# A hybrid attention / linear-recurrence step on one core: row sums traced in halves, eight casts moved to GpSimd, and eighteen products of the output projection listed inside the attention

## The chip, the cores and the metric

The kernel runs on one core of one Trainium2 chip. The core has five engines that run beside each other and are joined by semaphores: TensorE (PE, matrix products; PEld is its weight load), VectorE (DVE), ScalarE (ACT), GpSimd (POOL) and SyncE (SP, which here only issues DMAs). Every engine works its instructions off in the order of its own queue. [...]

The metric is the device time of one launch in microseconds. Three runs of the kernel before gave 846.48, 842.91 and 846.51 us, median 846.48.

## The reference, cut to what matters

Two layers work on 640 tokens: 512 latent tokens and 128 context tokens. Layer 0 is gated attention, layer 1 a gated linear recurrence. The change touches layer 0 and the hand-over to layer 1.

```python
# layer 0 (attention), for context (p) and latent (s) tokens
sh, sc, g = split(silu(cond) @ ada_w[0] + ada_b[0], 3)      # per-layer shift, scale, gate
h = x * (1 + sc) + sh
q, k, v, gate = split(h @ attn_w_in, [1024, 1280, 1536])     # 16 heads of 64, 4 key/value heads
q, k = rms_norm(q), rms_norm(k)                              # and rotary positions for s
p = softmax(q k^T / 8); o = p v                              # s reads 128 cached + 512 own keys
out = (o * silu(gate)) @ attn_w_out                          # the output projection, 1024 x 1024
x = layer_norm(ALPHA * x + g * out)
# layer 1 (recurrence) begins with its own modulation
sh, sc, g = split(silu(cond) @ ada_w[1] + ada_b[1], 3)
h1 = x * (1 + sc) + sh
```

All matrix products are made to nearly fp32 accuracy out of three products of reduced operands: an operand `x` is split into `hi = round(x)` and `lo = x - hi`, and `x w` becomes `hi hi + hi lo + lo hi`.

## The kernel before, in words

**Tiles.** 640 tokens are five tiles of 128 (tile 4 is the context). A width of 1024 is eight blocks `k` of 128. Activations `hhi`, `hlo` lie with the features on the partitions; after the attention the same two tiles hold the split, gated attention output.

**Weights.** Every weight piece is 128 x 1024, loaded by SP into a ring of three raw buffers (`rawp`), at most two pieces ahead (`pump`, L197). `split_piece` (L232) turns it into `hi` (L240, a cast on ACT) and `lo` (L241, a subtraction with two SBUF inputs, on DVE for all pieces that matter here). The loads are pinned: SP issues them in the order of the program, and one that waits for a buffer holds up all later ones.

**Order of the work.** All up to the output projection's weights stands in one block (L168 to L1248) that a list scheduler orders: for each engine it picks, at each simulated time, among the instructions whose inputs are there and whose buffers are free. `keep_in_program_order` pins an instruction behind the one traced before it on its engine. `issue_after(ins)` adds an order edge to `ins` from each instruction of its body that is on the engine of `ins`.

**Lead-in** (`lead_in`, L753). After keys, values and the first of four query chunks, 16 steps (L846 to L864) make the gate columns `gs`: each step is a half tile of 24 products (`gps`, L349 to L351) and a SiLU on ACT (L854). Beside them run the first chunk's query work (`q_job`: `qn` L615, rotary L654 to L658, split `qs` L693 and L694, transposes `qps` L702) and the *row sums* (`ada_cols`, L331): layer 1's shift and scale are 16 jobs, each of two DVE instructions (L335) that multiply a 128 x 1024 piece of `ada_w` with a row of silu(cond) and sum along the row. Twelve jobs run in the lead-in, one a step, from a ring of two buffers (`adar`, loads L840), their products spilled into `gs`; four run in `cols_gen` (L340) beside the first later query chunk, from `rawp`, spilled into the ring `s2` of two buffers that `q_split` (L689) takes its tiles from as well.

**Attention** (`att_gen`, L1001). 36 units, nine for each of four chunks `c`: eight sample units (one head, 256 queries) and one prompt unit. A unit's front (L959) is four score products (`sc`, L869 and L870), a maximum on DVE (L964), an exponential on ACT (L969) and, some steps later, a reciprocal on DVE (L974) and the scaling of the probabilities on POOL (L975). Its back is ten transposes (L982), copies out of PSUM (L874), and for two units together 20 products with the values (`pot`, L896) and the gating on DVE (L901). Fronts run two units ahead. The side work (`Side`, L60) is woven in at 0.62 steps per step of the attention: query chunks 1 to 3 (`q_gen`, L713) with the row sums or the gate rows (`ada_gen`, L315, products `adaps` L284), then the split of the first four output pieces (`prefetch_gen`, L1117) and the split of the attention output (`split_gs`, L1109).

**Output projection and first norm.** `out_mms` (L1153) makes 24 products of 128 x 512 for a token tile and a half `nh` of the columns; the loop at L1387 runs tiles and halves as (0,0), (1,0), (0,1), (1,1), (2,0), ... `Norm.half` (L1170) multiplies by the gate, adds the residual and takes statistics, `Norm.finish` scales, `h1_tile` (L1250) transposes the tile for layer 1. The PSUM pool of this phase (`Phase(4, 0)`, L1141) takes over the banks of the attention's pools.

Of the kernel before, what the change touches and what calls it, by code (L numbers as in the profile page):

```python
# [22 lines left out]
TT = 5  # L23
# [15 lines left out]
EARLY = 2  # L39
WARM = (8, 2, 3)  # L40
# [93 lines left out]
def hybrid_step(ctx: ExitStack, tc: tile.TileContext, a: dict, o: dict):  # L134
# [97 lines left out]
    def split_piece(hi, lo, src, lo_eng=None, after=()):  # L232
# [4 lines left out]
        with ExitStack() as st:  # L237
            for ins in after:
                st.enter_context(tc.issue_after(ins))
            nc.scalar.copy(hi, raw)  # L240
# [12 lines left out]
    class Weights:  # L253


        def __init__(self, name, c, engs=None, after=()):
            self.h, self.l = [], []
            for i in range(2):
                hi = wtile([P, 1024], F32R, tag="whi", name="whi")
                lo = wtile([P, 1024], F32R, tag="wlo", name="wlo")  # L260
                split_piece(hi, lo, (name, c, i), engs and engs[i], after)
# [69 lines left out]
    def ada_cols(job, raw, spill):  # L331

        s, ft = job
        for c in range(2):
            nc.vector.scalar_tensor_tensor(spill, raw, 1.0, silb[:, c, :], ALU.mult, ALU.mult,  # L335
                                           accum_out=shsc[1][:, s, ft, c:c + 1])
# [376 lines left out]
    def q_gen(c, X, fill):  # L713

        w = Weights("attn_w_in", c, (nc.vector, nc.vector), tuple(last_split))
# [37 lines left out]
    def lead_in(att):  # L753
# [89 lines left out]
        for _ in range(2):  # L843
            cols_load()
        step = 0
        for ch in range(6, 10):  # L846
# [3 lines left out]
            for mt in range(2):  # L850
                for j, (t0, t1) in enumerate(HALVES):
                    ps = bank_any("gps")
                    feat_mms(ps, w, mt, j, hhi, hlo)
                    nc.scalar.activation(gs[:, 2 * (ch - 6) + mt, t0:t1], ps[:, :320], AF.Silu)  # L854
# [10 lines left out]
        assert not raws  # L865


    def score_mms(out, X, c, h, t0, k0, k1):
        nc.tensor.matmul(out, X[:, h, t0:t0 + P], kk[:, c, k0:k1], start=True, stop=False)  # L869
        nc.tensor.matmul(out, X[:, h, t0:t0 + P], klo[:, c, k0:k1], start=False, stop=True)  # L870
# [22 lines left out]
    def av_mms(pot, slot, c, moving, first, last):  # L893

        for j in (1, 0):
            nc.tensor.matmul(pot[j * HD:(j + 1) * HD, :CW], vv[:, slot, c * HD:(c + 1) * HD], moving[j], start=first, stop=last)  # L896
# [58 lines left out]
    def sample_unit(c, h, qh):  # L955
# [22 lines left out]
        def trans(k0, m):  # L978
            pt = bank1("pt")
            for i in range(m):  # L980
                for q in range(2):
                    nc.tensor.transpose(pt[:, i * 256 + q * P:i * 256 + (q + 1) * P],  # L982
# [793 lines left out]
```

## Time and profile before

| what | value |
| --- | --- |
| median of the runs (lowest to highest) | 846.48 us (842.91 to 846.51) |
| the profiled execution's own time | 844.78 us |
| its span, first to last instruction | 843.0 us |
| mean granted clock of TensorE | 0.99 |
| TensorE busy | 808.0 us, 96% of the span |
| DVE, ACT, POOL busy | 559.9, 386.5, 215.8 us |
| attention ends, output projection begins | at 336.8 us of the span |

The page is one execution. Times are microseconds from the start of the span. A row of the time line or of a group reads: start, duration, engine, line, operation, what it writes <- what it reads, shape, count; in brackets the idle time of the engine before it and what ended it. A row of the windows reads: from:to, length, then the busy time and count of PE, PEld, DVE, ACT and POOL, the granted clock, the share of the DMA engines and GB/s. Rows with x2 or more are merged neighbours. TensorE's busy time is modelled for pipelined products, so neighbours overlap a little. Three stages can be told apart: the lead-in up to 143 us, the attention up to 336.8 us, and the output projection and layer 1 behind it.

### The profile page before, as it was taken

What the parts mean: (1) busy time and instruction counts of PE and PEld (TensorE: products, weight loads), DVE (VectorE), ACT (ScalarE), POOL (GpSimd) and SP (SyncE); (2) the same over time, 40 slices, a digit from 0 to 9 for tenths busy, and PEclk for the clock granted to TensorE, in tenths of its full rate; (3) what the DMA queues carried; (4) which work ended last, traced back from release to release, by engine and by line L of the source; (5) the groups of instructions that cost most, each with busy time, mean ns of one, the idle gap of its engine ahead of it and who ended that gap; (6) DMA issues with size and microseconds to landing.
All of it is one profiled execution on the core that took longest, in us unless ns stands there. A gap on an engine that the chain in (4) does not pass through costs nothing.

```text
span 843.0 us, 19206 instructions
## 1 busy us (share of the span) xinstructions
PE 808.0 (96%) x8025; PEld 729.2 (87%) x8025; DVE 559.9 (66%) x996; ACT 386.5 (46%) x782; POOL 215.8 (26%) x261
## 2 busy tenths in 40 slices
PE   8999899989999988999999999999999999999994
PEld 6789799878878766888999999999999999998774
DVE  4568882795657674776438575767668575858477
ACT  2252354674656776222434444435434544445232
POOL 0123001443344833010001304143333314121121
PEclk9999899999999999999999999999999999999998
DMA  9944451114151230630322322231322312324041
GB/s 325 397 145 165 151 175 52 51 54 148 51 200 51 101 100 1 225 125 35 108 69 68 103 72 82 83 109 51 107 89 83 99 61 89 120 65 157 23 161 75
DMA packets 34326, 93.28 MB, mean 111 GB/s; under 512 B 5040, under 2 KB 12224, under 8 KB 34240
## 3 DMA queue, kind: packets, MB, share of 16 engines
q1 hardware_dynamic: 23568, 74.10, 25.9%
q0 software_dynamic: 4768, 14.18, 5.4%
q10 hardware_dynamic: 5904, 3.78, 1.5%
q8 instruction: 63, 1.03, 0.5%
q14 instruction: 23, 0.19, 0.1%
HBM read 82.85 MB, written 9.19 MB: 109 GB/s over the span
## 4 chain that ended last, share of the span: by engine, by line
PE 82%; DVE 9%; ACT 2%; DMA 2%; issue 2%; POOL 1%; SPq 0%; DVEq 0%; ACTq 0%; POOLq 0%
PE rps L1319 7%; PE rps L1320 7%; PE rps L1321 7%; PE vgps L1309 5%; PE vgps L1311 5%; PE vgps L1310 5%; PE pot L896 4%; PE outp L1158 4%; PE outp L1160 3%; PE outp L1159 3%; PE pt L982 3%; PE lv L1452 2%; PE acc L536 2%; PE gps L349 2%; PE sc L869 2%
## 5 line engine op out<-in xcount | busy, mean ns | idle before, releaser
L1319 PE MATMUL rps<-h1hi,rhi 128*128 128x320 f32 x368 | 118.4, 322 | 0.0
L1320 PE MATMUL rps<-h1lo,rhi 128*128 128x320 f32 x368 | 113.9, 309 | 0.0
L1321 PE MATMUL rps<-h1hi,rlo 128*128 128x320 f32 x368 | 113.8, 309 | 0.0
L975 POOL TENSOR_SCALAR p<-p,rc 128x640 f32<-128x640 f32 x64 | 58.8, 921 | 116.6 <-DVE rc L974 102.3
L1319 PEld LDWEIGHTS rps<-h1hi,rhi 128*128 128x128 f32 x368 | 69.2, 188 | 1.3
L1320 PEld LDWEIGHTS rps<-h1lo,rhi 128*128 128x128 f32 x368 | 69.3, 188 | 0.0
L1321 PEld LDWEIGHTS rps<-h1hi,rlo 128*128 128x128 f32 x368 | 69.1, 188 | 0.0
L241 DVE TENSOR_TENSOR rlo<-raw,rhi 128x1024 fp32r<-128x1024 f32 x32 | 45.0, 1409 | 33.8 <-ACT rhi L240 33.8
L964 DVE TENSOR_REDUCE nm<-sc 128x1 f32<-128x640 f32 x64 | 52.0, 818 | 23.2 <-PE sc L870 22.8
L1480 POOL COPY At<-near 32x160 f32<-32x160 f32 x32 | 14.0, 438 | 196.8 <-DVE near L1442 195.8
L969 ACT ACTIVATE p<-sc,nm 128x640 f32<-128x640 f32 x64 | 51.2, 802 | 27.2 <-DVE nm L964 19.3
L240 ACT CAST rhi<-raw 128x1024 fp32r<-128x1024 f32 x32 | 33.6, 1049 | 52.0 <-PE rps L1320 48.8
L1430 ACT COPY kc<-A 128x640 f32<-128x640 f32 x40 | 32.2, 806 | 54.4 <-DVE A L1461 50.5
L1309 PE MATMUL vgps<-rhi,h1hi 128*128 128x256 f32 x180 | 51.5, 286 | 0.0
L1310 PE MATMUL vgps<-rlo,h1hi 128*128 128x256 f32 x180 | 50.9, 283 | 0.0
L1311 PE MATMUL vgps<-rhi,h1lo 128*128 128x256 f32 x180 | 50.9, 283 | 0.0
L982 PE MATMUL pt<-small,p 128*128 128x128 f32 x320 | 48.6, 276 | 1.4 <-ACT pts L874 0.9
L869 PE MATMUL sc<-kk,X 128*128 128x320 f32 x128 | 42.6, 343 | 6.1 <-ACT p L969 6.0
L874 ACT COPY pts<-pt 128x512 f32<-128x512 f32 x64 | 35.8, 591 | 24.4 <-PE pt L982 24.1
L982 PEld LDWEIGHTS pt<-small,p 128*128 128x128 f32 x320 | 37.1, 140 | 7.8 <-issue 5.3
L1309 PE MATMUL vgps<-wspare,h1hi 128*128 128x256 f32 x140 | 41.8, 298 | 0.0
L896 PE MATMUL pot<-pts,vv 128*64 128x256 f32 x320 | 38.9, 386 | 2.4 <-DVE pts L874 2.4
(301 smaller groups left out, 2423.6 us busy)
## 6 DMA issues: line engine op xcount, KB each, us to landing
raw<-in_rec_w_in SPq DMA_DIRECT2D x40, 512.0 KB, 3.7
raw<-in_ada_m SPq DMA_DIRECT2D x16, 512.0 KB, 8.0
raw<-in_attn_w_in SPq DMA_DIRECT2D x16, 512.0 KB, 4.2
raw<-in_ada_s SPq DMA_DIRECT2D x16, 512.0 KB, 4.4
adaraw<-in_ada_c SPq DMA_DIRECT2D x12, 512.0 KB, 3.8
raw<-in_attn_w_out SPq DMA_DIRECT2D x8, 512.0 KB, 4.1
raw<-in_rec_w_out SPq DMA_DIRECT2D x8, 512.0 KB, 3.5
x1d<-y SPq DMA_DIRECT2D x5, 512.0 KB, 2.6
```

Source lines behind the costliest of these rows:

```text
L869: nc.tensor.matmul(out, X[:, h, t0:t0 + P], kk[:, c, k0:k1], start=True, stop=False)
L896: nc.tensor.matmul(pot[j * HD:(j + 1) * HD, :CW], vv[:, slot, c * HD:(c + 1) * HD], moving[j], start=first, stop=last)
L964: nc.vector.tensor_reduce(nm[:, 0:1], sc[:, :, :320], AX.XY, ALU.max, negate=True)
L969: return nc.scalar.activation(halves(p[:]), sc[:, :, :320], AF.Exp, bias=nm[:, 0:1], accum_out=su[:, 0:1])
L975: nc.gpsimd.tensor_scalar(p, p, rs[:, 0:1], 1.0, ALU.mult, ALU.mult)
L982: nc.tensor.transpose(pt[:, i * 256 + q * P:i * 256 + (q + 1) * P], ps[q][:, (k0 + i) * P:(k0 + i + 1) * P], ident)
L1309: nc.tensor.matmul(out, h1hi[:, k, t], hi, start=(k == 0), stop=False)
L1310: nc.tensor.matmul(out, h1hi[:, k, t], lo, start=False, stop=False)
L1311: nc.tensor.matmul(out, h1lo[:, k, t], hi, start=False, stop=(k == KT - 1))
L1319: nc.tensor.matmul(ps[:, j, :320], hi[:, k, :], h1hi[:, k, t], start=(k == 0), stop=False)
L1320: nc.tensor.matmul(ps[:, j, :320], hi[:, k, :], h1lo[:, k, t], start=False, stop=False)
L1321: nc.tensor.matmul(ps[:, j, :320], lo[:, k, :], h1hi[:, k, t], start=False, stop=(k == KT - 1))
```

## The change

Five edits belong together:

1. **Row sums in halves.** `ada_cols` becomes a generator that yields after each of a job's two sums. In the lead-in one sum is traced a step in the first six steps and two a step from the seventh on, so the twelve jobs reach to step 15; sums traced behind the twelfth SiLU spill into the ring `s2` (`spare`), since the last steps write the place used so far. The load of a job's successor comes behind its second sum. Each sum is put under `issue_after` of the last SiLU. In `cols_gen` each sum yields and takes a spill tile of its own, under `issue_after` of the last query product.
2. **Eight casts on GpSimd.** `split_piece` takes the engine of the `hi` cast. It is GpSimd for the weights of query chunks 2 and 3 and for the first four pieces of the output projection; the subtraction stays on DVE.
3. **Order written out.** From the third unit before the end on, scores, transposes and value products are pinned on TensorE in the order of the program, and before the second to last unit the waiting value products are flushed first.
4. **Eighteen early products.** Tile 0, half 0 of the output projection, blocks `k` 0 to 5, is made in a PSUM buffer of the attention's pool: six products behind the second to last unit, four behind the last one, eight behind its value products. ACT copies the sum to SBUF (`part`), and `Norm.half` of that tile and half adds it.
5. **Phase change and order of tiles.** The PSUM pool of the projection is opened behind the scheduled block and waits tile by tile (`reuse_waits="tile"`) and not for the whole of the old pools. Tile 1 goes ahead of tile 0, and the two share PSUM buffers by halves.

```diff
-    def ada_cols(job, raw, spill):
+    def ada_cols(job, raw, spill, after):
         s, ft = job
         for c in range(2):
-            nc.vector.scalar_tensor_tensor(spill, raw, 1.0, silb[:, c, :], ALU.mult, ALU.mult,
-                                           accum_out=shsc[1][:, s, ft, c:c + 1])
+            with tc.issue_after(after()):
+                nc.vector.scalar_tensor_tensor(spill(), raw, 1.0, silb[:, c, :], ALU.mult, ALU.mult,
+                                               accum_out=shsc[1][:, s, ft, c:c + 1])
+            yield
...
+    def spare():
+        return prep.tile([P, D], F32, tag="s2", name="spill", bufs=2)
+
     def cols_gen():
         for job in COLS[len(COLS) - COLS_LATE:]:
-            ada_cols(job, take(("ada_c",) + job), prep.tile([P, D], F32, tag="s2", name="spill", bufs=2))
+            yield from ada_cols(job, take(("ada_c",) + job), spare, lambda: last_qmm[0])
             pump()
-            yield
...
+        def spill():
+            return gs[:, KT - 2:, :].rearrange("p a b -> p (a b)")[:, :D] if len(silus) <= 12 else spare()
+
+        def cols_steps():
+            while raws:
+                yield from ada_cols(*raws.popleft(), spill, lambda: silus[-1])
+                cols_load()
...
-                    if raws:
-                        ada_cols(*raws.popleft(), gs[:, KT - 2:, :].rearrange("p a b -> p (a b)")[:, :D])
-                        cols_load()
+                    for _ in range(1 if step < 7 else 2):
+                        next(cgen, None)
...
-            nc.scalar.copy(hi, raw)
+            (hi_copy or nc.scalar.copy)(hi, raw)
...
-        w = Weights("attn_w_in", c, (nc.vector, nc.vector), tuple(last_split))
+        w = Weights("attn_w_in", c, (nc.vector, nc.vector), tuple(last_split),
+                    nc.gpsimd.tensor_copy if c > 1 else None)
...
-        yield from wo_gen(0, PIECES[:4], woa[0])
+        yield from wo_gen(0, PIECES[:4], woa[0], nc.gpsimd.tensor_copy)
...
         for u, (c, _, back, end) in enumerate(units):
             fr = fronts(u + AHEAD)
+            left_over = len(units) - u
+            if left_over == 3:
+                listed[0] = True
+            if left_over == 2:
+                yield from flush()
...
+            if left_over < 3:
+                early_out(EARLY_OUT[2 - left_over])
+                yield
         yield from flush()
         while later:
             tick()
+        early_out(EARLY_OUT[2])
+        drain(early)
+        listed[0] = False
...
+    def early_mms():
+        ps = bank2("outq")[:, 0, :]
+        t = slice(0, P)
+        for k in range(6):
+            hi, lo = (w[:, k % 2, :] for w in wo[0, k // 2])
+            for x, w in ((hhi, hi), (hhi, lo), (hlo, hi)):
+                yield pin(nc.tensor.matmul(ps, x[:, k, t], w, start=(k == 0 and x is hhi and w is hi),
+                                           stop=(k == 5 and x is hlo)))
+        for n in range(2):
+            part.append(rowp.tile([P, CW], F32, tag="row", name="part"))
+            nc.scalar.copy(part[n], ps[:, n * CW:(n + 1) * CW])
+
+    def early_out(n):
+        side.finish()
+        for _ in range(n):
+            next(early)
...
-                pools["b2"] = self.st.enter_context(pool("b2", n2, space=PSUM))
+                pools["b2"] = self.st.enter_context(pool("b2", n2, space=PSUM, reuse_waits="tile"))
...
-    for tt, nh in ((0, 0), (1, 0), (0, 1), (1, 1), (2, 0), (2, 1), (3, 0), (3, 1), (4, 0), (4, 1)):
...
+    shared = [bank2("outp") for _ in range(2)]
+    for tt in (1, 0):
+        norms[tt] = Norm(tt, [t[:, 1 - tt, :] for t in shared])
+    for nh in range(2):
+        out_mms(norms[1].ps, 1, nh, hhi, hlo)
+        out_mms(norms[0].ps, 0, nh, hhi, hlo, range(0 if nh else 6, KT), first=0 if nh else 6)
...
```

`EARLY_OUT` is (6, 4, 8). The wrapper `listed_pe` around the score, transpose and value products pins them while `listed` is set.

More of the change, by code (lines that the diff above doesn't have):

```diff
@@ L230, in piece, with split_piece @@
         return a[name][c][:, i * 1024:(i + 1) * 1024]
[L232 removed]
+    def split_piece(hi, lo, src, lo_eng=None, after=(), hi_copy=None):
         pump()
@@ L253, in hybrid_step, with __init__ @@
     class Weights:
-        def __init__(self, name, c, engs=None, after=()):
+        def __init__(self, name, c, engs=None, after=(), hi_copy=None):
             self.h, self.l = [], []
@@ L260, in __init__ @@
                 lo = wtile([P, 1024], F32R, tag="wlo", name="wlo")
-                split_piece(hi, lo, (name, c, i), engs and engs[i], after)
+                split_piece(hi, lo, (name, c, i), engs and engs[i], after, hi_copy)
                 self.h.append(hi[:].rearrange("p (k n) -> p k n", k=4))
@@ L895, in av_mms @@
         for j in (1, 0):
-            nc.tensor.matmul(pot[j * HD:(j + 1) * HD, :CW], vv[:, slot, c * HD:(c + 1) * HD], moving[j], start=first, stop=last)
+            listed_pe(nc.tensor.matmul(pot[j * HD:(j + 1) * HD, :CW], vv[:, slot, c * HD:(c + 1) * HD], moving[j],
+                                       start=first, stop=last))
     def av_out(pot, gt):
@@ L1095, in hybrid_step, with wo_gen @@
     wo = {}
-    def wo_gen(layer, pieces, wpool):
+    part = []
+    def early_mms():
[9 more added lines that the diff above has]
+            nc.scalar.copy(part[n], ps[:, n * CW:(n + 1) * CW])
+    early = early_mms()
+    def early_out(n):
+        side.finish()
+        for _ in range(n):
+            next(early)
+    def wo_gen(layer, pieces, wpool, hi_copy=None):
         for nh, i in pieces:
@@ L1157, in out_mms @@
             hi, lo = (w[:, k % 2, c] for w in wo[nh, k // 2])
-            nc.tensor.matmul(out, ghi[:, k, t], hi, start=(k == 0), stop=False)
+            nc.tensor.matmul(out, ghi[:, k, t], hi, start=(k == first), stop=False)
             nc.tensor.matmul(out, ghi[:, k, t], lo, start=False, stop=False)
@@ L1162, in hybrid_step, with __init__ @@
     class Norm:
-        def __init__(self, tt):
-            self.tt, self.ps = tt, bank2("outp")
+        def __init__(self, tt, banks=None):
+            if banks is None:
+                both = bank2("outp")
+                banks = [both[:, nh, :] for nh in range(2)]
+            self.tt, self.ps = tt, banks
             self.x = lnp.tile([P, D], F32, tag="x", name="x", bufs=2)
```

58 lines of the change are left out of this document (38 added, 20 removed).

## The prediction

> **What bounds the kernel now.** I read the page first (spans, then the chain that ended last), then the waits of TensorE, then windows of 5 us, then the time line of the few windows where TensorE idles.
>
> ```profile
> span 843.0 us, 19206 instructions
> PE 808.0 (96%) x8025; PEld 729.2 (87%) x8025; DVE 559.9 (66%) x996; ACT 386.5 (46%) x782; POOL 215.8 (26%) x261
> PE 82%; DVE 9%; ACT 2%; DMA 2%; issue 2%; POOL 1%; SPq 0%; DVEq 0%; ACTq 0%; POOLq 0%
> ```
>
> TensorE is the bound: busy 808 of 843 us and 82% of the chain. No product is removed by the change, so it can win only idle time, 35 us in all, and time lost to a lower clock. It can lose by making new idle time. Columns of the next rows: window, busy time of PE, PEld, DVE, ACT, POOL, then granted clock, DMA share, GB/s.
>
> ```profile
> 85.00:90.00 5.00, 1.40 (x10) 1.14 (x8) 5.00 (x9) 1.05 (x2) 0.00 (x0) 0.87 0.33 109
> 90.00:95.00 5.00, 4.45 (x20) 4.29 (x21) 5.00 (x10) 1.69 (x3) 0.00 (x0) 0.50 0.57 207
> 150.00:155.00 5.00, 3.33 (x22) 2.54 (x20) 5.00 (x15) 2.99 (x7) 2.73 (x3) 1.00 0.06 22
> 180.00:185.00 5.00, 3.49 (x30) 2.84 (x30) 4.72 (x14) 5.00 (x11) 3.17 (x4) 1.00 0.04 13
> 295.00:300.00 5.00, 3.50 (x23) 2.51 (x21) 5.00 (x7) 4.71 (x9) 0.00 (x0) 1.00 0.47 138
> 300.00:305.00 5.00, 3.37 (x28) 2.60 (x30) 3.79 (x9) 4.21 (x9) 2.37 (x3) 1.00 0.75 237
> 324.00:337.00 13.00, 11.07 (x83) 7.83 (x84) 6.42 (x16) 7.90 (x18) 4.65 (x6) 1.00 0.01 1
> 337.00:360.00 23.00, 23.00 (x106) 19.11 (x107) 16.06 (x22) 6.20 (x7) 2.25 (x4) 1.00 0.68 229
> ```
>
> The reader sees four places: 85 to 95 (idle and a clock of 0.50), 150 to 185 (DVE full), 295 to 305 (ACT and DVE full, POOL idle), and the end of the attention, 324 to 337. From 337 on TensorE is full: what is won ahead of it reaches the end undiminished, and a later product there costs nothing while its inputs are early.
>
> **The change part by part.** *1. Row sums of the lead-in (L335).* In the first block a scheduler orders each engine's queue; only SP's loads are pinned as written.
>
> ```profile
> 82.45 0.69 DVE L615 TENSOR_TENSOR qn<-pmm,rq 128x512 f32<-128x512 f32 x1 [0.85 <-POOL rq L191]
> 83.06 1.21 DVE L335 SCALAR_TENSOR_TENSOR gs<-adaraw,silb 128x1024 f32<-128x1024 f32 x1
> 85.40 1.22 DVE L335 SCALAR_TENSOR_TENSOR gs<-adaraw,silb 128x1024 f32<-128x1024 f32 x1
> 87.75 1.22 DVE L335 SCALAR_TENSOR_TENSOR gs<-adaraw,silb 128x1024 f32<-128x1024 f32 x1
> 89.49 0.69 DVE L694 TENSOR_TENSOR qs<-r,qs 128x512 fp32r<-128x512 f32 x1
> 90.33 1.23 PE L702 MATMUL qps<-identr,qs 128*128 128x128 f32 x8 [3.92 <-DVE qs L694]
> 91.78 0.64 PE L349 MATMUL gps<-hhi,whi 128*128 128x320 f32 x1 [0.22 <-ACT X L704]
> 95.78 0.31 PE L349 MATMUL gps<-hhi,whi 128*128 128x320 f32 x1
> 96.22 0.31 PE L349 MATMUL gps<-hhi,whi 128*128 128x320 f32 x1
> 76.05 13.28 SPq L840 DMA_DIRECT2D adaraw<-in_ada_c  x4
> 89.38 8.68 SPq L219 DMA_DIRECT2D raw<-in_attn_w_in  x2
> ```
>
> Three sums stand between qn and qs of the first query unit, and TensorE waits 3.92 us for qs. Then five groups of three products take 91.78 to 95.78, 4.00 us, where a group at full clock takes 0.44 (95.78 to 96.22): 4.00 - 5 x 0.44 = 1.80 us lost to the clock. The new order edge is drawn by the library only to instructions on the engine of the instruction named; a sum is on DVE and the half tile's SiLU on ACT, so I count the hold itself as nothing. What moves is SP's order: with one sum a step, two steps go to a job, so behind the first two loads only one more column load stands ahead of the pair of weight loads that ends at 98 (89.38 + 8.68), where now four do. The fourth job's sums, in order those of 85.40 and 87.75, have no data before that. They leave the chain: 1.14 us each to the next start, 2.3 us. Of the wait 3.92 - 2.3 = 1.6 us stays; the window 150 to 155, with 1.67 us idle in it, kept a clock of 1.00, so the 1.80 us go too. Term: -4.1 us. Bounds: 0 (the sums stay) and -5.9 (3.92 + 0.22 + 1.80: all gone). The late sums fall into 97 to 137, beside gate products, where the waits of TensorE show none on DVE; each one that it did wait for would cost 1.2 us; SP's pinned queue then has the loads of query chunk 1 behind fewer column loads and the last four column loads behind more, both wanted only after 140.
>
> *2. Row sums of the first query chunk.* Four jobs of two sums run at 144 to 187, and now each half takes a buffer of its own from the ring of two that the query splits use.
>
> ```profile
> 157.10 1.75 DVE L335 SCALAR_TENSOR_TENSOR spill<-raw,silb 128x1024 f32<-128x1024 f32 x1
> 157.35 0.61 ACT L693 CAST qs<-qn 128x512 fp32r<-128x512 f32 x1
> 182.68 1.40 DVE L335 SCALAR_TENSOR_TENSOR spill<-raw,silb 128x1024 f32<-128x1024 f32 x1
> 182.78 0.43 ACT L693 CAST qs<-qn 128x256 fp32r<-128x256 f32 x1
> 185.48 1.21 DVE L335 SCALAR_TENSOR_TENSOR spill<-raw,silb 128x1024 f32<-128x1024 f32 x1
> 190.11 0.64 PE L284 MATMUL adaps<-raw,sil 128*32 128x256 f32 x8 [1.15 <-DMA raw<-in_ada_s]
> ```
>
> A job's first sum starts within 0.3 us of the query split ahead of it in the ring, so the ring's order holds it. With halves, three come ahead of the third split and five behind it (182.8), where now two do. DVE has 1.2 us less before 155 and 3.6 us more from 183 on; the buffers of three jobs come free later, and with them chunk 2's weights and the gate rows that TensorE already awaits for 1.15 us. Behind a full DVE I take -1 us at 150 to 155 and +2 at 183 to 195. Term: +1.0 us. Bounds: -1.2, and +8.4 if the five sums keep the 2.8 us spacing of 182.68 to 185.48 (the fifth starts at 182.68 + 4 x 2.8 = 193.9 and not 185.48) and nothing covers the later loads.
>
> *3. Eight casts from ACT to POOL* (weights of chunks 2 and 3, the first four output pieces).
>
> ```profile
> 299.75 1.04 ACT L240 CAST wohi<-raw 128x1024 fp32r<-128x1024 f32 x1 [0.28 <-DMA raw<-in_attn_w_out]
> 300.67 0.80 POOL L975 TENSOR_SCALAR p<-p,rc 128x640 f32<-128x640 f32 x1 [6.09 <-DVE rc L974]
> 301.63 0.41 PE L869 MATMUL sc<-kk,X 128*128 128x320 f32 x1 [1.71 <-ACT p L969]
> L975 POOL TENSOR_SCALAR p<-p,rc 128x640 f32<-128x640 f32 x64 | 58.8, 921 | 116.6 <-DVE rc L974 102.3
> 289.17 2.52 DVE L694 TENSOR_TENSOR qs<-qn,qs 128x256 fp32r<-128x256 f32 x1
> 289.85 1.55 POOL L1107 TENSOR_TENSOR hlo<-gs,hhi 128x640 fp32r<-128x640 f32 x1
> 291.84 0.50 PE L702 MATMUL qps<-identr,qs 128*128 128x128 f32 x4 [1.02 <-DVE qs L694]
> ```
>
> ACT loses 8 x 1.04 us. No row shows a POOL cast: 1024 columns at the rate of L975 (0.921 us for 640) are 1.5 us, at that of L1107 2.5 us (two inputs); I take 1.5, one input being nearer. Four such fit the 6.09 us that POOL idles ahead of 300.67. TensorE's score products waited there for exponentials behind casts: idle in 295 to 305 is 1.50 + 1.63 = 3.1 us, of which I take two thirds back. The casts of 183 stand in a window with 1.51 us idle, left for part 2; those of 229 and 236 meet no wait. The edges behind the last query split no longer bind the casts of chunks 2 and 3, since they name ACT and DVE; the casts can only come earlier for it. What queues behind a POOL cast is the scaling of probabilities (L975), two units ahead of its transposes, so hidden; without that lead each cast costs its 1.5 us. Term: -2.0 us. Bounds: -4.6 (3.1 + 1.51) and +4.1: at 289.17 a 256-column DVE operation with two SBUF inputs lasted 2.52 us beside POOL, against 0.69 for 512 columns at 89.49, and TensorE paid 1.02; four output casts, each with its DVE subtraction, would pay that four times. [...]
>
> *4. Eighteen early products, pinned order, waits by tile.*
>
> ```profile
> 327.04 0.42 PE L869 MATMUL sc<-kk,X 128*128 128x320 f32 x1
> 333.92 2.38 PE L896 MATMUL pot<-pts,vv 128*64 128x256 f32 x20 [0.52 <-DVE pts L874]
> 336.82 0.51 PE L1158 MATMUL outp<-wohi,hhi 128*128 128x512 f32 x1 [0.53 <-DVE gs L901]
> 343.12 0.39 PE L1158 MATMUL outp<-wohi,hhi 128*128 128x512 f32 x1
> 343.80 0.39 PE L1158 MATMUL outp<-wohi,hhi 128*128 128x512 f32 x1
> ```
>
> A product takes (343.80 - 343.12) / 3 = 0.227 us, 18 of them 4.1 us, taken from after 336.82 and put before it. Idle time there is 13.00 - 11.07 = 1.9 us, the 0.53 us for the last gating (L901) included, which waits by tile remove. The order now written out puts all eight transposes of a unit ahead of the next scores, which the scheduler mixed (the last ones at 327.04, between two groups of transposes), so I allow 1.0 us of new idle. Term: -0.9 us; bounds -1.9 and +1.1. Two 256-column copies and two additions come to ACT and DVE, DVE at 16 of 23 us in 337 to 360, so hidden; uncovered they would be 2 us. Tile 1 now goes ahead of tile 0 with the same products on a full TensorE (23.00 of 23.00), which costs nothing while its inputs are early: the second half's weights are wanted after 30 products and not after 48, but those 30 start some 3 us later (4.1 - 0.9), so 48 - 30 - 14 = 4 products, 0.9 us, of their lead go, and that much it would cost if they had none.
>
> *Sum.* -4.1 + 1.0 - 2.0 - 0.9 = -6.0 us on the profiled execution's 844.78 us: 838.8. That execution lies 1.7 us under the median of the runs (846.48); 0.5% of it is 4.2 us, about what a measurement of this kernel can tell from no change, so faster means under 842.2 and slower over 850.7.
>
> **The rivals.** *No shorter chain in the lead-in:* the hold binds nothing and the scheduler fills DVE with sums as before, part 1 is 0: 842.9. For it: sums fill every pause of DVE from 82 to 96. Against it: the fourth job's load.
> *The tail of five row sums behind the third query split.* Part 2 at its +8.4, and the clock's 1.8 us with it, since the waits around it would pass the 3.92 us after which it fell: 838.8 + 7.4 + 1.8 = 848.0. Against it: attention units of chunk 1 need no weights of chunk 2 and can fill TensorE.
> *Slower: POOL and DVE hold each other up at every moved cast.* With the four output casts at the 1.02 us of 291.84 each, part 3 is +4.1: 844.9. If all eight hold DVE as at 289.17 (2.52 us, where half of the 0.69 of 89.49 is 0.35: 2.2 us more) and TensorE waits for all of it, part 3 is 8 x 2.2 = +17.6: 840.8 + 17.6 = 858.4. Without part 3's -2.0 the sum is 840.8, and 850.7 is 9.9 us above it: it decides from 9.9 / 8 = 1.24 us of waiting for each cast. For it the one row of 2.52 us; against it that 64 scalings on POOL raise no such wait elsewhere, and that the weights are wanted long after the casts.
> *More than forecast:* all four lower bounds, -13.6: 831.2.
>
> **How the numbers follow.** Forecast 0.50 (its own range 834 to 842); more than forecast 0.10; lead-in unchanged 0.13; tail of row sums 0.11; POOL in the way at four casts 0.04, at all eight 0.12. Faster 0.50 + 0.10 = 0.60, within 0.13 + 0.11 + 0.04 = 0.28, slower 0.12. The range leaves out the far end of the best case and the slowest one: 832.5 to 849.
>
> **What would show it.** Part 1: the wait of qps for qs near 1.6 us, the clock near 1.0 in 85 to 95, six sums before it and none from 88 to 97. Part 2: five sums after the third split, first gate-row product later than 190. Part 3: casts on POOL near 1.5 us, the score products' waits between 290 and 305 at most a third, no DVE subtraction over 2 us. Part 4: first product after the attention without a wait, idle in its last 13 us near 1. It is wrong if idle time merely moves: if 140 to 337 keeps its share of idle, only parts 1 and 4 are left.

## The result

The changed kernel runs in 851.26 us (median of six runs, 849.25 to 853.90) against 845.13 us for the kernel before beside it (six runs). The ratio is 1.0079, with a 95% interval of 1.0052 to 1.0105: about 6 us slower, where 838.8 was forecast and 849 was the upper end of the range. The profiled execution took 853.24 us. First its page: span, engines, and the shares of the chain that ended last.

```profile
span 851.4 us, 19216 instructions
PE 812.2 (95%) x8025; PEld 730.8 (86%) x8025; DVE 563.5 (66%) x998; ACT 379.9 (45%) x776; POOL 228.4 (27%) x269
PE 82%; DVE 9%; issue 2%; ACT 2%; DMA 2%; POOL 1%; SPq 0%; DVEq 0%; ACTq 0%; POOLq 0%
```

TensorE makes the same 8025 products and takes 4.2 us more for them (812.2 against 808.0), and it idles 39.2 us where it idled 35.0. Both halves of the 8.4 us between the two spans have to be found. The windows of the changed kernel show where (columns as before: PE, PEld, DVE, ACT, POOL, granted clock, DMA share, GB/s).

```profile
85.00:90.00 5.00, 3.15 (x26) 2.92 (x24) 4.86 (x10) 0.97 (x3) 0.00 (x0) 1.00 0.00 0
90.00:95.00 5.00, 4.61 (x23) 4.46 (x22) 1.37 (x2) 2.62 (x4) 0.00 (x0) 0.66 0.01 2
150.00:155.00 5.00, 3.58 (x26) 2.71 (x28) 5.00 (x16) 3.14 (x8) 3.54 (x3) 1.00 0.00 0
180.00:185.00 5.00, 4.64 (x37) 3.24 (x36) 4.79 (x12) 3.63 (x9) 4.17 (x4) 1.00 0.12 34
185.00:190.00 5.00, 2.38 (x18) 1.85 (x16) 5.00 (x10) 1.96 (x4) 4.01 (x3) 0.94 0.43 143
190.00:195.00 5.00, 1.67 (x8) 1.23 (x12) 5.00 (x9) 0.89 (x2) 3.44 (x4) 0.50 0.37 143
195.00:200.00 5.00, 5.00 (x33) 3.76 (x25) 1.71 (x5) 0.59 (x1) 0.29 (x1) 0.54 0.83 288
335.50:348.50 13.00, 12.50 (x88) 9.23 (x87) 5.24 (x12) 7.05 (x14) 3.55 (x5) 1.00 0.00 1
```

The lead-in (85 to 95) is better, as forecast. The attention now ends at 348.5 us and not at 336.8; in its last 13 us TensorE idles 0.5 us where it idled 1.9. The loss stands at 185 to 200: 5.95 us of idle time in the first ten, DVE full, and a clock of 0.50 in which the next products run. In the time line of that stretch, DVE's row sums (L337), the maximum that waits among them (L986), the loads (L220), the GpSimd casts (L241), their subtractions (L242) and the products that wait for them read:

```profile
181.95 1.20 DVE L337 SCALAR_TENSOR_TENSOR spill<-raw,silb 128x1024 f32<-128x1024 f32 x1
183.19 4.87 SPq L220 DMA_DIRECT2D raw<-in_attn_w_in  x2
184.21 1.22 DVE L337 SCALAR_TENSOR_TENSOR spill<-raw,silb 128x1024 f32<-128x1024 f32 x1
186.48 1.21 DVE L337 SCALAR_TENSOR_TENSOR spill<-raw,silb 128x1024 f32<-128x1024 f32 x1
186.99 1.59 POOL L241 CAST whi<-raw 128x1024 fp32r<-128x1024 f32 x1 [0.99 <-DMA raw<-in_attn_w_in]
187.62 2.04 DVE L337 SCALAR_TENSOR_TENSOR spill<-raw,silb 128x1024 f32<-128x1024 f32 x1
189.59 0.81 DVE L986 TENSOR_REDUCE nm<-sc 128x1 f32<-128x640 f32 x1
190.40 1.20 DVE L337 SCALAR_TENSOR_TENSOR spill<-raw,silb 128x1024 f32<-128x1024 f32 x1
191.46 0.63 PE L890 MATMUL sc<-kk,X 128*128 128x320 f32 x1 [3.00 <-ACT p L991]
191.64 5.47 SPq L220 DMA_DIRECT2D raw<-in_ada_s  x4
192.22 1.03 POOL L241 CAST whi<-raw 128x1024 fp32r<-128x1024 f32 x1
192.27 2.06 DVE L242 TENSOR_TENSOR wlo<-raw,whi 128x1024 fp32r<-128x1024 f32 x1
194.76 1.08 PE L285 MATMUL adaps<-raw,sil 128*32 128x256 f32 x8 [1.86 <-DMA raw<-in_ada_s]
```

Five sums stand from 181.95 on, where before two did. A raw buffer is given back when its job's second sum has ended: chunk 2's weights are issued at 183.19, behind the sum that ends at 183.15, and the gate rows' pieces at 191.64, behind the fifth sum (190.40 + 1.20). In the kernel before these two loads went out 22 and 5 us earlier, the first behind a sum that ended at 160.65:

```profile
159.44 1.21 DVE L335 SCALAR_TENSOR_TENSOR spill<-raw,silb 128x1024 f32<-128x1024 f32 x1
160.69 16.82 SPq L219 DMA_DIRECT2D raw<-in_attn_w_in  x2
186.72 8.32 SPq L219 DMA_DIRECT2D raw<-in_ada_s  x5
```

Meanwhile the maximum of a unit waits in DVE's queue between sums, its exponential behind it, and the score products wait 3.00 us for that. In 175 to 210 TensorE waits 4.7 us in all for exponentials and 1.9 for the gate rows' load; before it was 1.3 and 1.2.

### The profile page after: what moved, and what is told of

Its sections match the earlier page's. It is cut to its first block, busy times and chain, and to the rows that moved or that the text cites. A ratio compares the mean times of both kernels' runs of the same rounds, so it can differ in the third digit from the quotient of the medians.

```text
span 851.4 us, 19216 instructions
## 1 busy us (share of the span) xinstructions
PE 812.2 (95%) x8025; PEld 730.8 (86%) x8025; DVE 563.5 (66%) x998; ACT 379.9 (45%) x776; POOL 228.4 (27%) x269
## 4 chain that ended last, share of the span: by engine, by line
PE 82%; DVE 9%; issue 2%; ACT 2%; DMA 2%; POOL 1%; SPq 0%; DVEq 0%; ACTq 0%; POOLq 0%
PE rps L1383 7%; PE rps L1384 7%; PE rps L1385 7%; PE vgps L1373 5%; PE vgps L1375 4%; PE vgps L1374 4%; PE pot L917 4%; PE pt L1004 3%; PE outp L1212 3%; PE outp L1214 3%; PE outp L1213 3%; PE acc L541 2%; PE lv L1525 2%; PE sc L890 2%; PE gps L354 2%
## 5 line engine op out<-in xcount | busy, mean ns | idle before, releaser
L997 POOL TENSOR_SCALAR p<-p,rc 128x640 f32<-128x640 f32 x64 | 63.3, 992 | 111.8 <-DVE rc L996 107.3
L242 DVE TENSOR_TENSOR rlo<-raw,rhi 128x1024 fp32r<-128x1024 f32 x32 | 45.1, 1409 | 34.1 <-ACT rhi L241 34.0
L986 DVE TENSOR_REDUCE nm<-sc 128x1 f32<-128x640 f32 x64 | 52.0, 816 | 13.3 <-PE sc L891 12.8
L241 ACT CAST rhi<-raw 128x1024 fp32r<-128x1024 f32 x32 | 33.6, 1049 | 52.2 <-PE rps L1384 49.3
L354 PE MATMUL gps<-hhi,whi 128*128 128x320 f32 x128 | 40.6, 317 | 0.4 <-ACT X L709 0.4
```

What stands on the lines that cost most here:

```text
L354: nc.tensor.matmul(ps[:, :320], w.hi(k)[:, c], hhi[:, k, t], start=(k == 0), stop=False)
L986: nc.vector.tensor_reduce(nm[:, 0:1], sc[:, :, :320], AX.XY, ALU.max, negate=True)
L997: nc.gpsimd.tensor_scalar(p, p, rs[:, 0:1], 1.0, ALU.mult, ALU.mult)
```

## The experiments

All times are set against the kernel before on the same chip. Beside the ratio I read each trace at four places: the first gate product (72.17 us before, 73.29 after), the first query product of chunk 1 (141.20 and 139.77), that of chunk 3 (243.19 and 249.74), and the first product of layer 1's projection (410.90 and 419.31). The differences between these landmarks, less those of the kernel before, say in which stage the time went. The time to the first of them differs by up to 2.2 us either way, which I take for noise of the loads, and after the last the traces run alike within 0.8 us. There is one trace of each kernel, and a stage can differ by chance: the changed kernel and run 11, whose instructions stand in the same order, differ by 1.9 us in the lead-in. In the table, "lead-in" is 72 to 141, "chunks 1, 2" is 141 to 243, and "chunk 3, end" is 243 to 411, all in us against the kernel before.

| kernel | us | ratio (95% interval) | lead-in | chunks 1, 2 | chunk 3, end |
| --- | --- | --- | --- | --- | --- |
| changed | 851.26 | 1.0079 (1.0052 to 1.0105) | -2.55 | +7.98 | +1.86 |
| 1: whole jobs | 847.93 | 1.0053 (1.0033 to 1.0073) | -2.74 | +4.76 | +1.87 |
| 2: casts on ACT | 851.84 | 1.0098 (1.0076 to 1.0120) | -2.54 | +7.76 | +1.92 |
| 3: both of these | 841.01 | 0.9970 (0.9954 to 0.9987) | -2.49 | -0.27 | -0.26 |
| 4: before, halves | 852.70 | 1.0114 (1.0087 to 1.0140) | -0.52 | +7.86 | +1.90 |
| 5: two sums a unit | 842.39 | 0.9961 (0.9942 to 0.9981) | -2.38 | -0.16 | -0.24 |
| 6: query casts | 845.26 | 1.0005 (0.9986 to 1.0025) | -2.44 | +3.61 | -0.23 |
| 7: before, early products | 843.87 | 0.9984 (0.9962 to 1.0006) | -0.14 | -0.38 | -0.27 |
| 8: before, lead-in | 840.47 | 0.9949 (0.9925 to 0.9973) | -3.94 | -0.35 | -0.10 |
| 9: casts behind the root | 843.65 | 0.9977 (0.9955 to 0.9999) | -3.99 | +1.50 | -0.47 |
| 10: output casts | 840.16 | 0.9932 (0.9907 to 0.9957) | -2.77 | -0.24 | -2.22 |
| 11: no hold | 852.52 | 1.0080 (1.0050 to 1.0111) | -0.64 | +8.48 | +1.25 |
| 12: before, lead-in, output casts | 838.69 | 0.9939 (0.9919 to 0.9960) | -3.59 | -0.08 | -2.21 |

Two theories stood at the start. "Tail": the five row sums behind the third query split are the loss. "Casts on GpSimd": the moved casts are, through DVE (the sum of 2.04 us and the subtraction of 2.06 us run beside a cast).

### 1. Whole jobs again

```diff
-            yield from ada_cols(job, take(("ada_c",) + job), spare, lambda: last_qmm[0])
-            pump()
+            raw, t = take(("ada_c",) + job), spare()
+            drain(ada_cols(job, raw, lambda: t, lambda: last_qmm[0]))
+            pump()
+            yield
```

> The changed kernel with one part undone: in the first later query chunk a job's two row sums are traced in one step with one spill tile again (three jobs ahead of the third query split, one behind). All else stays. Theory 'tail': the five sums behind the third split cost the 6.7 us that TensorE's stream loses between 172 and 197 us (it is 1.24 us ahead of before's at 172 and 5.44 us behind at 196), so this kernel gives 851.3 - 6.7 = 844.6 us, the third query chunk's first product comes near 190 and the clock stays at 1.00 in 185 to 200. Theory 'casts on GpSimd': the casts at 187 and 192 hold DVE up (a sum of 2.04 us, a subtraction of 2.06 us) and the scaling of probabilities with them; undoing the halves then changes little: 849 to 851, and the clock still falls there.

Measured 847.93. That is neither: the first query product of chunk 2 comes at 190.51, as the tail theory has it, but 4.76 us are lost in chunks 1 and 2 all the same, and the granted clock still falls to 0.50 in 188 to 194.

### 2. Casts on ACT again

```diff
-                    nc.gpsimd.tensor_copy if c > 1 else None)
+                    None)
...
-        yield from wo_gen(0, PIECES[:4], woa[0], nc.gpsimd.tensor_copy)
+        yield from wo_gen(0, PIECES[:4], woa[0])
```

> The changed kernel with the eight casts on ACT again, all else kept. Theory 'tail': no gain at 185 to 200, 850 to 852 us; at 290 to 320 at most 1 us either way. Theory 'casts on GpSimd': the stretched sum and subtraction go (2 x 0.85 us) with the waits and the lowered clock around them: 844 to 846 us, and the products of the third query chunk begin before 192.

Measured 851.84: nothing gained. With the halves in place the casts cost nothing in addition, against the second theory.

### 3. Both undone

> The changed kernel with both undone: whole jobs in the first later query chunk, all eight casts on ACT. What is left is the lead-in's halves, the early products and the written order. By the landmarks of the two traces these are worth -2.5 us (lead-in) and about 0 (end): 842.5 to 843.5 us. Theory 'tail' has it within 2 us of the run with whole jobs alone; theory 'casts on GpSimd' has it within 2 us of the run with the casts on ACT alone; if the two need each other, either single undoing already gives this time.

Measured 841.01, 2.5 us under the kernel before (0.0030 x 843.25), which is the lead-in's landmark. So the casts alone cost 7.0 us (run 1 against this one, 0.0083 x 843), the halves alone 9.6 (run 4, below), and both together 9.2 (0.0109 x 845, the changed kernel against this one): no more than one of them. Each alone makes its pause in the same stretch, ahead of the gate rows near 190 (runs 4 and 6 below), which would explain it: together they spend one pause. Neither theory in its pure form is right.

### 4. The halves alone, on the kernel before

```diff
-            ada_cols(job, take(("ada_c",) + job), prep.tile([P, D], F32, tag="s2", name="spill", bufs=2))
-            pump()
-            yield
+            (s, ft), raw = job, take(("ada_c",) + job)
+            for c in range(2):
+                nc.vector.scalar_tensor_tensor(prep.tile([P, D], F32, tag="s2", name="spill", bufs=2), raw, 1.0,
+                                               silb[:, c, :], ALU.mult, ALU.mult,
+                                               accum_out=shsc[1][:, s, ft, c:c + 1])
+                yield
...
```

> The kernel before with one part of the change alone: in the first later query chunk each row sum has a step and a spill tile of its own, as in the changed kernel; the lead-in, the casts (ACT) and the end stay as before. Theory 'tail': 845.1 + 6.7 = 851.8 us, five sums behind the third split, the third query chunk's products from 196 on, clock near 0.5 in 190 to 200. Theory 'casts on GpSimd': the five sums alone cost little, 845 to 847 us.

Measured 852.70, a loss of 9.6 us (0.0114 x 843.25), with no cast on GpSimd. Windows of this run (columns as above), then TensorE's waits in 175 to 200 (total, times, longest):

```profile
185.00:190.00 5.00, 1.81 (x8) 1.20 (x7) 5.00 (x8) 3.00 (x6) 0.47 (x1) 0.80 0.33 107
190.00:195.00 5.00, 2.86 (x17) 1.65 (x16) 4.08 (x11) 1.04 (x1) 2.53 (x2) 0.50 0.80 263
195.00:200.00 5.00, 5.00 (x33) 4.46 (x33) 0.42 (x1) 0.59 (x1) 0.00 (x0) 0.67 0.43 160
```

```profile
PE sc L876 <- ACT p L976: 3.5, 3, 2.4
PE adaps L284 <- DMA raw<-in_ada_s: 2.1, 1, 2.1
```

The reader sees the same picture as in the changed kernel: DVE full while TensorE starves, score products behind exponentials, gate rows behind their load. Of the loss in chunks 1 and 2 only part is idle time: TensorE idles 6.13 us in 175 to 210 and 1.10 in 210 to 280 here, 3.16 and 0.36 before (35 and 70 less its busy time in these windows). That is +3.7 of +7.86 us. About as much goes with the lower clock: by the means of the three windows above (0.80, 0.50 and 0.67) it was at 0.50 for some 10.3 us (2.0 + 5.0 + 3.3, if it was 1.00 otherwise), and TensorE was busy 6.2 to 8.0 us of them (2.86 + 3.3, and at most the 1.81 of the first window). In the prediction's rows of the lead-in the low clock cost 1.80 of 4.00 us, 45%; at that rate I estimate 2.8 to 3.6 us here. The further 1.9 us in chunk 3 and the end come in the changed kernel and in runs 1, 2 and 4, and 1.25 us in run 11. Over 280 to 352 the mean clock was 0.98 in the changed kernel and run 1 and 0.95 in runs 2 and 4; in run 11 it was 1.00 and the time was lost all the same, so the cause is open.

### 5. Two sums a unit

```diff
             next(fill, None)
             yield
+            if c == 1:
+                next(fill, None)
             yield
```

> Casts on ACT, halves kept, but the query generator takes two sums a unit from the first later chunk's generator and not one: six sums (each with a step and a spill tile of its own) then stand ahead of the third query split and two behind it, as with whole jobs. Theory 'count': the loss comes from the number of sums behind the third split, so this gives the time of whole jobs, 841 to 843 us, with the clock at 1.00 in 185 to 200. Theory 'buffers': a spill tile for every half ties the sums to the ring of two that the query splits use, whatever their number; then 846 to 852 us remain.

Measured 842.39, and -0.16 us in chunks 1 and 2, where run 2, the same kernel without this edit, has 851.84 and +7.76: with halves, a tile for each half, and the ring of two as they are, the loss is gone once six sums stand ahead of the third split. It is the count, not the buffers.

### 6. Only the query casts on GpSimd

Run 1 with the output casts back on ACT (the second hunk of run 2).

> Whole jobs; on GpSimd only the four casts of the query weights, the four of the output weights on ACT. The run with all eight was at 847.9, with none at 841.0. Theory 'query casts': the loss is at 172 to 210, where TensorE had nothing to do from 185.3 to 188.7 and a clock of 0.50 behind it: 3.7 to 4.8 us are kept, 845 to 846 us, and the pair of 280 to 352 us (1.8 us) goes. Theory 'output casts': the four casts at 300 are the ones: 842 to 843 us.

Measured 845.26, 3.0 us over run 3 (0.0035 x 845), all of it in chunks 1 and 2. The reason is in run 1, whose instructions are the same up to there. Its rows in the time line are the input of a query unit's reciprocal root (DVE), the second cast, the root (L192, on GpSimd too), the cast's load and that of the gate rows, and the product that waits for the latter.

```profile
174.59 0.33 SPq L220 DMA_DIRECT2D raw<-in_attn_w_in  x1
177.00 0.15 DVE L191 TENSOR_SCALAR rs_t<-ss 128x4 f32<-128x4 f32 x1
178.38 1.05 POOL L241 CAST whi<-raw 128x1024 fp32r<-128x1024 f32 x1 [2.84 <-PE pt L1006]
179.38 1.03 POOL L192 TENSOR_TENSOR rstd<-rs_t,mhalf 128x4 f32<-128x4 f32 x1
185.44 4.76 SPq L220 DMA_DIRECT2D raw<-in_ada_s  x4
188.73 1.08 PE L285 MATMUL adaps<-raw,sil 128*32 128x256 f32 x8 [3.42 <-DMA raw<-in_ada_s]
```

The same load among the DMA issues of that stretch (KB each, us to landing):

```profile
raw<-in_attn_w_in SPq DMA_DIRECT2D x1, 512.0 KB, 3.7
```

The cast's weights were issued at 174.59 and landed 3.7 us later, at 178.3; until then the cast stood at the head of GpSimd's queue with nothing running. The root's input was there at 177.15, the root ran at 179.38. The normalized query, the third split, the last sums and the gate rows' load come as much later, and TensorE waits 3.42 us where it waited 1.15 (3.2 us in run 6's own trace).

### 9. The same casts behind the root

```diff
-        nc.gpsimd.tensor_tensor(out, t[:, :n], mhalf[:, :n], ALU.pow)
+        last_rstd[:] = [nc.gpsimd.tensor_tensor(out, t[:, :n], mhalf[:, :n], ALU.pow).ins]
...
-        w = Weights("attn_w_in", c, (nc.vector, nc.vector), tuple(last_split),
+        w = Weights("attn_w_in", c, (nc.vector, nc.vector), tuple(last_split) + tuple(last_rstd),
```

> Whole jobs and the four query casts on GpSimd, as in the run of 845.3 us, with one order edge more: a cast stands behind the last reciprocal root of the query chunk ahead (both on GpSimd, so here the edge binds). In the run with whole jobs and all casts on GpSimd, a cast that waited for its weights stood ahead of that root: the root's input was there at 177.15, the cast ran from 178.38, the root from 179.38, 2.2 us late, and the third split, the last row sums and the loads of ada_s came as much later. Theory 'queue': the 3 us of the query casts go, 842 to 843 us, no clock below 1.00 in 185 to 200, TensorE's wait for ada_s near 1.1 us and not 3.4. Theory 'contention' (DVE and GpSimd slow each other whenever a cast runs): the cost stays, 844.5 to 846 us.

Measured 843.65, a ratio of 0.9977 where run 6 had 1.0005 and run 3 0.9970. Input, root and casts, then TensorE's wait for the gate rows:

```profile
176.90 0.16 DVE L193 TENSOR_SCALAR rs_t<-ss 128x4 f32<-128x4 f32 x1
177.14 1.02 POOL L194 TENSOR_TENSOR rstd<-rs_t,mhalf 128x4 f32<-128x4 f32 x1 [2.06 <-DVE rs_t L193]
178.12 2.22 POOL L243 CAST whi<-raw 128x1024 fp32r<-128x1024 f32 x2
```

```profile
PE adaps L287 <- DMA raw<-in_ada_s: 0.7, 2, 0.5
```

The root starts when its input is there, the longest wait is 0.5 us and not 3.42, and TensorE's clock is 1.00 all through 175 to 210. The casts run as before beside DVE. So the queue was the larger part of the cost. It is not shown to be all of it: the time lies between the two theories, nearer the first. By the ratios 2.4 of 3.0 us come back, each figure good to about 2.5 us. By the traces 2.1 of 3.9 us come back in chunks 1 and 2 (+3.61 to +1.50, with -0.27 in run 3); the 1.8 us left there may be DVE and GpSimd in each other's way or chance. Late in the attention the trace has a stretch of lowered clock besides:

```profile
290.00:300.00 10.00, 7.46 (x46) 0.86 0.30 89
```

### 10. Only the output casts on GpSimd

> Whole jobs, query casts on ACT, the four output casts alone on GpSimd. The run with all eight less the run with the query casts is 2.7 to 4 us. If the two groups add up, this is 841.0 + 3.4 = 844.4 us, with idle time and a lowered clock near 300 to 310. If the output casts only cost through the shift that the query casts make, it is 841 to 842 us.

Measured 840.16: not a loss but a gain, 3.2 us by the ratios (0.0038 x 845) and 1.96 us by the landmarks against run 3. The window over the end of the attention, run 3 first, then this run:

```profile
280.00:352.00 72.00, 65.38 (x452) 49.79 (x449) 45.87 (x85) 45.99 (x94) 29.44 (x34) 1.00 0.28 92
```

```profile
280.00:352.00 72.00, 67.14 (x455) 51.93 (x454) 48.45 (x87) 41.99 (x89) 32.48 (x36) 1.00 0.30 103
```

Idle time falls by 1.76 us. Run 12 against run 8 shows the same gain (-2.21 against -0.10). Beside the query casts the same four casts lose: chunk 3 and the end stand at +1.87 in run 1, which has all eight, and at -0.23 in run 6, which has the query casts alone. Up to 1.6 of these 2.1 us, estimated by the same 45%, go with some 3.5 us at a clock of 0.50 in run 1 (means of 0.82 in 300 to 305 and 0.83 in 305 to 310), where run 6 has 1.00 over 280 to 352; the changed kernel has 0.77 in 310 to 315. Runs 2 and 4, whose casts are on ACT, have a lowered clock there as well (0.95 over 280 to 352), so how much of it belongs to the casts isn't settled.

### 7, 8 and 12. The other parts alone

Run 7 is the kernel before with the written order, the early products, the waits by tile and the order of tiles; run 8 is the kernel before with the lead-in's halves (the diff of the change for `ada_cols`, `cols_steps` and the loop, with whole jobs in `cols_gen`); run 12 is run 8 with the four output casts on GpSimd.

> The kernel before with the written order, the early products, the waits by tile and the order of tiles alone (lead-in, row sums and casts as before). The landmarks of the run with whole jobs and casts on ACT put it at -0.25 us: 845 less 0.25, within 0.3% of the kernel before. The prediction's step gave -0.9 (from -1.9 to +1.1).

> The kernel before with the lead-in's halves alone. The landmarks put the lead-in at -2.5 us in three traces (idle -1.9, clock -0.9): a ratio near 0.997. If the order of SP's loads is the cause, DVE has one sum between qn and the last column loads and TensorE's wait for qs falls from 3.9 to about 1.9 us. If the hold were the cause, taking its edges away would change the order of DVE's instructions; the compiled order of all five engines is the same with and without them.

> The kernel before with two parts alone: the lead-in's halves and the four output casts on GpSimd; no early products, no written order, row sums of the first later chunk as whole jobs. Theory 'the early products are worth nothing': the same as the run of 840.16 us, which has them too, a ratio of 0.993 (0.991 to 0.996). Theory 'they are worth their -0.9 us': 841 us, 0.9943. Theory 'they cost' (the lead-in alone stood at 0.9949, with the early products beside it at 0.997): 838.5 us, 0.991. The interval of such a run is about 0.0025 to either side, so only the last against the first could be told apart, and barely.

Run 7 gave 0.9984: the end alone is worth -1.4 us, with an interval from -3.2 to +0.5; its trace has -0.27 in the stage where the edit acts. Run 8 gave 0.9949, -4.3 us, where 0.997 was expected: in its trace the clock stays at 1.00 through the lead-in (72 to 137), while its mean there was 0.97 in the three traces behind that figure. Run 12 gave 0.9939 without the early products, run 10 0.9932 with them: what they are worth there can't be told apart from nothing. Runs 10 and 12 beat both kernels.

### 11. No hold

```diff
-            with tc.issue_after(after()):
+            if True:
```

> The changed kernel without the order edges of its row sums. Compiled, all five engines have the same instructions in the same order as in the changed kernel. Theory 'no-op': the time of the changed kernel, 851 us, within 0.3%, and the same waits of TensorE. What the trace also tells: whether the stretches of lowered clock (0.66 in 90 to 95, 0.50 in 190 to 197, 0.89 in 310 to 320) come again where the instructions are the same.

Measured 852.52, ratio 1.0080, the changed kernel's 1.0079: the hold does nothing. Since the instructions are the same, the two traces also show what is chance: TensorE's wait for the first `qs` is 1.85 us in one and 2.69 in the other. Windows of the changed kernel, then of run 11 (here PE, clock, DMA share, GB/s):

```profile
90.00:95.00 5.00, 4.61 (x23) 0.66 0.01 2
310.00:320.00 10.00, 8.54 (x58) 0.89 0.43 155
```

```profile
90.00:95.00 5.00, 5.00 (x27) 0.63 0.01 3
310.00:320.00 10.00, 7.81 (x57) 1.00 0.42 134
```

The lowered clock at 185 to 200 came in both. That near 310 came in one of them, with no more idle time in 310 to 320 than in the other (1.46 us against 2.19).

## Why the prediction was wrong

**Part 1, the lead-in: the wait was right, the clock half luck.** Forecast -4.1, measured alone -4.3 (0.9949, interval -6.3 to -2.3), in its trace -3.94. No sum stands between 85.3 and 95 in the changed kernel. The rows of the first query unit there:

```profile
83.51 0.69 DVE L620 TENSOR_TENSOR qn<-pmm,rq 128x512 f32<-128x512 f32 x1 [0.93 <-POOL rq L192]
84.11 1.22 DVE L337 SCALAR_TENSOR_TENSOR gs<-adaraw,silb 128x1024 f32<-128x1024 f32 x1
88.54 0.69 DVE L699 TENSOR_TENSOR qs<-r,qs 128x512 fp32r<-128x512 f32 x1
89.38 0.84 PE L707 MATMUL qps<-identr,qs 128*128 128x128 f32 x8 [1.85 <-DVE qs L699]
```

One sum is left between `qn` and `qs`, the wait is 1.85 us (forecast 1.6). The hold is nothing, as counted. What is not a constant is the -1.8 us of clock inside the term: with a wait of 1.85 us (runs 8 and 9) or 2.2 us (run 12) the clock stayed at 1.00 in 90 to 95, and the lead-in gained 3.6 to 4.0 us. In the other eight traces with this lead-in the clock fell (0.95 to 0.97 over 72 to 137, against 1.00 in runs 8, 9 and 12), in the changed kernel to a mean of 0.66 there behind the same 1.85 us, and 0.6 to 2.8 us were gained. The argument from 150 to 155, that an idle 1.67 us kept the clock, does not carry over.

**Part 2, the row sums of the first query chunk: this step failed.** The count of five was right, and so were the later loads. The sentence that failed is "Behind a full DVE I take -1 us at 150 to 155 and +2 at 183 to 195": measured alone it is +9.6 us, against a bound of +8.4 and, with the clock, the rival's +10.2. The rival named the mechanism and was put aside for a wrong reason, that "attention units of chunk 1 need no weights of chunk 2 and can fill TensorE". They need no weights, but each unit needs DVE for its maximum, and a DVE that is full with sums holds their exponentials up. What fills TensorE was itself behind the engine that had the tail. That the rival's +10.2 is so near is partly luck: it counted late loads and 1.8 us of clock, and the trace of run 4 has 3.7 us of idle time, by the estimate there 2.8 to 3.6 of clock, and 1.9 in a later stage that are not explained. Which of the two chains weighs more, maxima behind sums or loads behind sums, was not separated by a run; by the waits in 175 to 210 of the changed kernel the maxima do (+3.4 us against +0.7).

**Part 3, the casts: half right, half of the wrong sign.** Forecast -2.0 for eight; measured +7.0 (run 1 against run 3) where the sums are whole jobs. The output casts did what was forecast only with the query casts on ACT (run 10: 1.76 us less idle time, of a forecast 2 of 3.1); beside the query casts, as in the change, run 1 against run 6 has them lose. For the query casts the failed sentence is "What queues behind a POOL cast is the scaling of probabilities (L975), two units ahead of its transposes, so hidden". The list of what queues there was not complete: the reciprocal root of the query norm is on GpSimd too, and it has no lead: the third split, the last sums and the gate rows' load hang on it. "The casts can only come earlier" was true, and that was the harm: an early cast waits for its weights at the head of the queue (in run 1 it ran from 178.38 and the root behind it from 179.38, with the root's input there at 177.15). The cast itself is 1.04 us, not 1.5. Longer rows of DVE beside a GpSimd cast are there in the changed kernel, the sum of 2.04 us and the subtraction of 2.06 us, against medians of 1.21 and 1.22; no run here shows by what they are held up. But by run 9 the larger part of the query casts' cost was the queue, so the rival "each cast holds DVE up" can name at most the rest.

In the changed kernel no cast stands ahead of that root: the halves delay the weights' load to 183.19, and the root ran from 179.87.

**Part 4, the end: not told apart from nothing.** Forecast -0.9; run 7 gives -1.4 with an interval that includes both that and nothing, its trace -0.27. In the last 13 us of the attention the idle time falls as forecast, to 0.5 us in the changed kernel. But part of it moves on. The prediction has TensorE full from 337 on and lets a later product cost nothing there; in the changed order a product of the projection waits for a PSUM buffer until the norm (`y`, on DVE) has read it. Run 7, TensorE's waits in 366 to 400, where the kernel before has none:

```profile
PE outp L1216 <- DVE y L1241: 0.8, 1, 0.8
```

The changed kernel has the same wait of 0.8 us. So the step that failed is that a product behind 337 costs nothing.

**The sum.** The terms, measured alone, are -4.3, +9.6, about 0 for casts beside halves (run 2), and -1.4: +3.9 us. Measured together it is +6.1 by the medians and +6.7 by the ratio. The difference is within the intervals (each term has about 2 us to either side). The changed kernel's trace also shows one part of it: the lead-in gave 2.55 us there, at a mean clock of 0.66 in 90 to 95, and not 3.94.

## What to carry to other kernels

Before an instruction is moved to an idle engine, list everything on that engine's queue behind the place where it will stand, small operations first, and ask what it waits for there: a move that lets it be issued early lets it block early. Cover is no cover when it runs through the engine that has become full; follow a covering unit through every engine that it needs. When steps are cut into halves in a generator that is called a fixed number of times, count how many fall behind the last call.

## What the runs showed of the hardware that was not expected

- **A lowered clock came with the pause.** Of the 7.86 us that the halves cost in chunks 1 and 2 of run 4, an estimated 2.8 to 3.6 are products at a lowered clock in and behind the pause (0.50 in 190 to 195, 0.67 in 195 to 200). In the attention of the kernel before no wait passes 1.71 us, 7.45 of 10 us are busy in 180 to 190, and the clock stays at 1.00.
- **The same wait did not bring the same clock.** The wait for `qs` was 1.85 us in the changed kernel and in run 8, and the clock fell in the first alone. The windows around the wait (PE, clock, DMA share, GB/s), first in the changed kernel:

```profile
85.00:90.00 5.00, 3.15 (x26) 1.00 0.00 0
90.00:95.00 5.00, 4.61 (x23) 0.66 0.01 2
```

The same in run 8:

```profile
85.00:90.00 5.00, 2.75 (x21) 1.00 0.00 0
90.00:95.00 5.00, 5.00 (x39) 1.00 0.06 20
```

TensorE was busy less ahead of 90 in run 8, 2.75 us against 3.15, and its clock stayed at 1.00. What decides is not shown by these runs. The 0.66 is a mean: in the changed kernel's trace the clock was 0.50 from 90.42 to 93.83 and 1.00 from there to 97.24.
- **GpSimd casts as fast as ACT.** In the changed kernel 1024 columns of fp32 to fp32r took a median of 1.04 us there, 1.05 on ACT, and once, beside two of DVE's row sums, 1.59 us.
